# Two more feed-forward pairs by seven half-size products, and double scratch buffers between a pair's products

## The chip, the cores and the metric

The kernel runs on one core of one Trainium2 chip. The metric is the device time of one execution in microseconds (us); the median of three runs is 1425.7 us (1424.77 to 1426.21). The clock that the throttle granted to TensorE was 0.998 of full speed in the profiled execution.

## The reference

The program is a two-layer encoder trunk on 512 tokens of width 1024, in float32. Each layer is a mixer (attention in layer 0, an mLSTM in layer 1), a cross-attention to 256 memory rows, and a gated feed-forward stage with a short convolution. The change lies in the feed-forward stage alone:

```python
D_FF = 256 * math.ceil(8 * D_MODEL / 3 / 256)      # 2816
FFN_CONV = 3

def conv_ffn(xn, w_up, conv_w, conv_b, w_down):
    h = causal_depthwise_conv(xn @ w_up, conv_w) + conv_b
    g, u = jnp.split(h, 2, axis=-1)
    return (jax.nn.gelu(g) * u) @ w_down

# in each of the two layers:
x = x + conv_ffn(rms_norm(x, ffn_norm[layer]), ffn_w_up[layer], ffn_conv_w[layer],
                 ffn_conv_b[layer], ffn_w_down[layer])
```

## The kernel before

**Precision.** Every large product is made of three matmuls (`mm3`, lines 334 to 342): weight and input are each split into a rounded high part and the remainder, and high times high, high times low and low times high are added in PSUM. The high part of a weight is a cast on ScalarE (`wh`, `s2h`, `s4h`, `a22h`), the remainder a subtraction on VectorE (`wl`, `s2l`, `s4l`, `a22l`), from a tile that a DMA filled (`raw`, `sa`, `ra`) or that VectorE added up (`sb`).

**The feed-forward stage** (`ffn_steps`) walks over 22 pairs. Pair p is block p of the gate half and block 22+p of the linear half of the up-projection, 128 columns each, over 1024 input rows and 512 tokens. A pair ends in `tail`: three-tap convolution (one `c` activation on ScalarE and two `c<-hs,vec,c` on VectorE for each half), gelu, the product of both halves, and the split of the result into `ah` and `al`. The result is multiplied with the down-projection in chunks of 4, 4, 4, 4 and 6 pairs (`down`, tile `w`); from pair 5 on, two such down-products stand between a pair's own products (`fill`).

**Two ways to make a pair.** `plain` computes two blocks of 8 x 3 matmuls with 512 columns each, and VectorE scales each block on its way out (`hs<-acc,rb`). `seven` sees the pair as a product of 2 x 2 half-size blocks (two weight blocks, each in two halves of 512 rows, against two halves of the rows and of the tokens) and makes it from seven products instead of eight: each has 4 x 3 matmuls with 256 columns. It needs sums of weight blocks. The sum of the two weight blocks, `sa`, is made by a load from SP and an accumulating DMA from GpSimd onto it; `sb` is a sum on VectorE, onto which a second accumulating DMA adds once its split is made. It also needs sums of the input's blocks, `th` and `tl`, formed once a layer during pairs 0 and 1 (`forms`). Between the products, partial sums are taken out of PSUM: ScalarE copies the first product's bank to `v` and, after two more products have been added in that bank, to `u2` and `u3` (both are called `u` in the profile); VectorE adds these to other banks to get the four quarters of `hs`; one operation (`hs<-hs,rb`) then scales the whole pair. In the order of the code the seven are p1 (bank Y), p2 (X), p6 (onto Y), p5 (R), p7 (onto Y), p4 (onto Y), p3 (onto R). p6 needs `v` copied, p7 needs `u2`, p4 needs `u3`, and p3 needs the quarter that is made from `u3` and R.

**Order.** `Sched` is a planner: it is given each step with an engine, a duration, its inputs and the buffers that it takes, runs a timetable by its own durations, and issues the steps in that order. The order on VectorE and ScalarE is then fixed; the other engines take the instructions as issued. A name such as `v=1` in the planner's table is the count of buffers that it reckons with; the same count stands where the tile is made (`bufs`). `hs` has two buffers, `c` one, `sa` three, `sb` two, the weight parts `wh` and `wl` three.

Of the kernel before, what the change touches and what calls it, by code (L numbers as in the profile page):

```python
# [16 lines left out]
P = 128  # L17
# [5 lines left out]
NPAIR = DFF // P  # L23
CHUNKS = [(0, 4), (4, 4), (8, 4), (12, 4), (16, 6)]

SEVEN = (range(4, 22), range(4, 22))
EPS = 1e-6

X_AT, X_STEP = 2.6, 0.6
# [38 lines left out]
def folded(ap):  # L68

    return ap.rearrange("p (r k) -> p r k", r=2)  # L70
# [13 lines left out]
class Plan:  # L84
# [11 lines left out]
    def add(self, fn, dur=0.0, deps=(), prio=None, take=(), free=(), chain=(), pre=(), after=0.0, order=(), load=(), st=None):  # L96
        it = Item(fn, dur, [d for d in deps if d is not None], len(self.items) if prio is None else prio, take, free, chain, pre, after, order, load, st)
        it.n = len(self.items)
        self.items.append(it)
        return it  # L100
# [188 lines left out]
class Builder:  # L289
# [22 lines left out]
    def bank(self, tag):  # L312
        tag, bufs = BANKS[tag]
        return self.til(self.aux, tag, bufs=bufs)
# [918 lines left out]
    def ffn_steps(self, layer, mp):  # L1233
# [1 line left out]


        nc, t = self.nc, self.t
        sc = Sched(raw=3, h=3, s2=1, s4=1, a22=1, sa=3, sb=2, ra=2, hs=2, c=1, ft=2, v=1, u2=1, u3=1, act=10, acc=4, s=2, w=2)
        add = sc.add
        tt = lambda n: 0.055 + 1.06e-3 * n  # L1240
        act = lambda n: 0.1 + 0.83e-3 * n
# [195 lines left out]
        def seven(p, fill):  # L1437
            st, sa, sb, r2, f1, f3, s2, s4, a22 = ({} for _ in range(9))
# [57 lines left out]
            get = rows(st, at + 2.0)  # L1496

            def copied(tag, scale):
                st[tag] = self.til(mp, tag, (P, 256), bufs=1)
                nc.scalar.activation(folded(st[tag][:]), bank("Y")(), AF.Copy, scale=scale)  # L1500

            def sum_(out, a, b, op):
# [4 lines left out]
            hs = lambda j, l: (lambda: folded(st["hs_"][:, j, 2 + 256 * l : 258 + 256 * l]))  # L1507
            AC = 0.42
            p1 = pe(n, lambda: opened("Y", by, "acc", f3, 0, *X(0, 0), "Y", True), [w3], [("acc", by)])
            v = add("ACT", AC, lambda: copied("v", 1.0), [p1], clock[0], [("v", bv)])  # L1510
            p2 = pe(n, lambda: opened("X", bx, "acc", f3, 512, *X(1, 0), "X", True), [w3], [("acc", bx)], [("h", f3)])
            c11 = add("DVE", 0.33, lambda: sum_(hs(0, 0), bank("X"), tmp("v"), ALU.add), [p2, v, get], clock[0] + 2.0, (), [("acc", bx), ("v", bv)])
            p6 = pe(n, lambda: product(s2, 0, *T2, "Y", False), [w2, v, *formed], (), [("s2", s2)])
            u2 = add("ACT", AC, lambda: copied("u2", 1.0), [p6], clock[0], [("u2", bu2)])
            fill()
            p5 = pe(n, lambda: opened("R", br, "s", f1, 512, *T1, "R", True), [w1], [("s", br)])
            p7 = pe(n, lambda: product(f1, 0, *T3, "Y", False), [u2, w1], (), [("h", f1)])
            u3 = add("ACT", AC, lambda: copied("u3", -1.0), [p7], clock[0], [("u3", bu3)])
            c22 = add("DVE", 0.33, lambda: sum_(hs(1, 1), tmp("u3"), bank("R"), ALU.subtract), [u3, p5, get], clock[0], (), [("u3", bu3)])
            fill()  # L1520
# [52 lines left out]
        for p in range(22):  # L1573
            if p in due:
                queue += [(due[p], m) for m in range(8)]
            if p == 19:
                n = 6 if layer == 0 else 4
                queue, late = queue[:-n], queue[-n:]
            (seven if p in SEVEN[layer] else plain)(p, fill if p >= 5 else lambda: None)
            if p < 2:  # L1580
# [405 lines left out]
```

## Time and profile before

| what | value |
|---|---|
| median of 3 runs | 1425.7 us (1424.77 to 1426.21) |
| profiled execution | 1423.48 us, its span 1421.7 us |
| TensorE (PE) busy | 1403.3 us, 99% of the span |
| VectorE (DVE) busy | 1133.5 us, 80% |
| ScalarE (ACT) busy | 823.8 us, 58% |
| GpSimd (POOL) busy | 129.9 us, 9% |
| first matmul of the feed-forward of layer 0 / 1 | 397.37 us / 1085.38 us of the span |
| DMA | 190.02 MB, mean 134 GB/s |

PE's rows are matmuls, PEld's the weight loads beside them. Matmuls are pipelined, so the duration of one is longer than the distance to the next; the distance from start to start is what a matmul costs where nothing waits. The same holds for VectorE and ScalarE, where an instruction starts up to 0.1 us before the one ahead of it ends.

### The profile page before, as it was taken

To read this page: it belongs to the slowest core of one execution; us is meant where nothing else is said; L and a number is where in the kernel's file an instruction comes from. 1 tells how busy PE (TensorE), PEld (TensorE's weight loads), DVE (VectorE), ACT (ScalarE), POOL (GpSimd) and SP (SyncE) were. 2 spreads that over 40 slices of the span, in tenths; PEclk is the share of its full clock that TensorE was granted. 3 is DMA by queue.
4 is the path that set the end of the run, shared out by engine and by line. 5 is a ranking of instruction groups with operands and counts; after the bars stand their busy time and mean duration, and the time that the engine had idled before them with its cause. 6 is when DMAs were issued, how large, how long until landed. Compare 5 with 4: busy or idle time off the path is not lost.

```text
span 1421.7 us, 22241 instructions
## 1 busy us (share of the span) xinstructions
PE 1403.3 (99%) x8440; PEld 1262.9 (89%) x8440; DVE 1133.5 (80%) x1906; ACT 823.8 (58%) x1382; POOL 129.9 (9%) x189
## 2 busy tenths in 40 slices
PE   9999999999999999999999999999999999999998
PEld 7878788899889999999887788989988999999997
DVE  7778596666689999999768657667667999999984
ACT  7777574444476656566456654445445665656655
POOL 0001240000001111110001210000000111111000
PEclk9999999999999999999999999999999999999999
DMA  5233224323248777773233322323323886777522
GB/s 205 90 108 108 90 79 152 132 76 133 86 150 217 191 180 184 182 182 106 86 105 112 105 95 97 119 92 120 130 74 120 212 202 171 193 179 185 143 77 80
DMA packets 69211, 190.02 MB, mean 134 GB/s; under 512 B 7552, under 2 KB 7552, under 8 KB 69104
## 3 DMA queue, kind: packets, MB, share of 16 engines
q1 hardware_dynamic: 55648, 153.48, 32.3%
q0 software_dynamic: 12448, 34.00, 13.7%
q8 instruction: 66, 1.08, 0.3%
q10 hardware_dynamic: 1008, 1.12, 0.2%
q14 instruction: 41, 0.34, 0.1%
HBM read 186.43 MB, written 2.15 MB: 133 GB/s over the span
## 4 chain that ended last, share of the span: by engine, by line
PE 83%; DVE 8%; ACT 4%; issue 3%; DMA 1%; POOL 1%; SPq 0%; POOLq 0%; DVEq 0%; ACTq 0%
PE acc L340 16%; PE acc L341 16%; PE acc L342 16%; PE w L340 5%; PE w L342 5%; PE w L341 5%; PE s L340 3%; PE s L341 3%; PE s L342 3%; PE acc L402 2%; PE acc L404 2%; PE acc L403 2%; DVE wl L262 2%; DVE x L262 1%; PE w L1765 1%
## 5 line engine op out<-in xcount | busy, mean ns | idle before, releaser
L262 ACT CAST wh<-raw 128x1024 fp32r<-128x1024 f32 (+2 forms) x229 | 235.0, 1027 | 205.6 <-PE acc L341 118.8
L262 DVE TENSOR_TENSOR wl<-raw,wh 128x1024 fp32r<-128x1024 f32 (+2 forms) x229 | 274.2, 1198 | 38.7 <-ACT wh L262 38.2
L340 PE MATMUL acc<-xh,wh 128*128 128x512 f32 (+1 forms) x800 | 278.6, 348 | 0.8 <-ACT v L262 0.8
L341 PE MATMUL acc<-xl,wh 128*128 128x512 f32 (+1 forms) x800 | 274.0, 343 | 0.0
L342 PE MATMUL acc<-xh,wl 128*128 128x512 f32 (+1 forms) x800 | 273.6, 342 | 0.0
L340 PEld LDWEIGHTS acc<-xh,wh 128*128 128x128 f32 x800 | 152.5, 191 | 14.5 <-ACT v L262 1.2
L342 PEld LDWEIGHTS acc<-xh,wl 128*128 128x128 f32 x800 | 152.4, 190 | 13.9
L341 PEld LDWEIGHTS acc<-xl,wh 128*128 128x128 f32 x800 | 152.5, 191 | 13.2
L262 DVE SCALAR_TENSOR_TENSOR c<-hs,vec,c 128x512 f32<-128x512 f32 x176 | 131.8, 749 | 3.8 <-ACT c L262 0.8
L340 PE MATMUL w<-ah,wh 128*128 128x512 f32 x304 | 115.7, 381 | 0.2 <-ACT c L262 0.2
L342 PE MATMUL w<-ah,wl 128*128 128x512 f32 x304 | 115.2, 379 | 0.0
L341 PE MATMUL w<-al,wh 128*128 128x512 f32 x304 | 115.2, 379 | 0.0
L262 ACT ACTIVATE c<-hs,vec 128x512 f32<-128x512 f32 x88 | 70.8, 811 | 9.9 <-DVE hs L262 5.4
L262 ACT CAST ah<-c 128x512 fp32r<-128x512 f32 x44 | 27.2, 619 | 83.8 <-DVE c L262 83.8
L262 DVE TENSOR_TENSOR x<-acc,x 128x512 f32<-128x512 f32 (+1 forms) x43 | 28.1, 653 | 54.2 <-PE acc L342 53.4
L340 PEld LDWEIGHTS w<-ah,wh 128*128 128x128 f32 x304 | 57.6, 190 | 8.0 <-DVE x L262 0.9
L342 PEld LDWEIGHTS w<-ah,wl 128*128 128x128 f32 x304 | 57.5, 189 | 8.1
L341 PEld LDWEIGHTS w<-al,wh 128*128 128x128 f32 x304 | 57.6, 190 | 6.5
L342 PE MATMUL acc<-mem,wl 128*128 128x256 f32 (+1 forms) x192 | 59.9, 312 | 0.0
L340 PE MATMUL acc<-mem,wh 128*128 128x256 f32 (+1 forms) x192 | 59.6, 311 | 0.0
L341 PE MATMUL acc<-mem,wh 128*128 128x256 f32 (+1 forms) x192 | 59.6, 311 | 0.0
L1446 POOL DMA_DIRECT2D sa<-in_up_dram x36 | 30.8, 857 | 290.6 <-DMA sa<-in_up_dram 212.7
(357 smaller groups left out, 3750.5 us busy)
## 6 DMA issues: line engine op xcount, KB each, us to landing
raw<-in_up_dram SPq DMA_DIRECT2D x52, 512.0 KB, 3.7
sa<-in_up_dram SPq DMA_DIRECT2D x36, 512.0 KB, 3.4
sa<-in_up_dram POOLq DMA_DIRECT2D x36, 512.0 KB, 5.9
raw<-in_down_dram SPq DMA_DIRECT2D x32, 512.0 KB, 3.6
ra<-in_up_dram SPq DMA_DIRECT2D x36, 256.0 KB, 4.0
sb<-in_up_dram POOLq DMA_DIRECT2D x36, 256.0 KB, 4.9
raw<-in_xk_dram SPq DMA_DIRECT2D x16, 512.0 KB, 3.2
raw<-in_wo_dram SPq DMA_DIRECT2D x16, 512.0 KB, 3.3
```

The lines of the kernel that those rows point to most:

```text
L262: i = issue(*a, **k)
L340: mm(out, wh, xh, start=first, stop=False, skip_group_check=parts)
L341: mm(out, wh, xl, start=False, stop=False, skip_group_check=parts)
L342: mm(out, wl, xh, start=False, stop=last, skip_group_check=parts)
L402: mm(ps, xh[k][:, ts], wh, start=(k == 0), stop=False)
L403: mm(ps, xh[k][:, ts], wl, start=False, stop=False)
L404: mm(ps, xl[k][:, ts], wh, start=False, stop=(k == 7))
L1446: return add("POOL", 0.0029 * cols, lambda: nc.gpsimd.dma_start(out(), src(), accum_op=ALU.add), deps, due, (), (), 6.0)
L1765: nc.tensor.matmul(ps[:, lo:], vv[s][:, c], a[:], start=(s == 0), stop=(s == 3))
```

## The change

Pair 3 of both layers is made by `seven` instead of `plain`, so that pairs 3 to 21 are; pairs 0 to 2 stay. The tiles `v`, `u2` and `u3` get two buffers each, in the planner's table and where the tiles are made.

```diff
-SEVEN = (range(4, 22), range(4, 22))
+SEVEN = (range(3, 22), range(3, 22))
...
-        sc = Sched(raw=3, h=3, s2=1, s4=1, a22=1, sa=3, sb=2, ra=2, hs=2, c=1, ft=2, v=1, u2=1, u3=1, act=10, acc=4, s=2, w=2)
+        sc = Sched(raw=3, h=3, s2=1, s4=1, a22=1, sa=3, sb=2, ra=2, hs=2, c=1, ft=2, v=2, u2=2, u3=2, act=10, acc=4, s=2, w=2)
...
             def copied(tag, scale):
-                st[tag] = self.til(mp, tag, (P, 256), bufs=1)
+                st[tag] = self.til(mp, tag, (P, 256), bufs=2)
```

The planner makes a new order from this. It differs from the old one from pair 3 to about pair 10 of each layer and is the same everywhere else; the two layers change alike.

**PE, layer 0, from the end of pair 2 on.** Before, the rows are these, the first row of each product and the last of pair 2; `acc_907` and `acc_915` are the two plain blocks of pair 3, `acc_922`, `acc_926` and `s_4589` the banks Y, X and R of pair 4, `acc_939` the bank Y of pair 5.

```order
L342 MATMUL acc_899_4396<-xh_835_4097,wl_4319 128x512
L340 MATMUL acc_907_4441<-xh_794_3875,wh_4366 128x512
...
L340 MATMUL acc_915_4486<-xh_794_3875,wh_4412 128x512
...
L340 MATMUL acc_922_4528<-xh_794_3875,wh_4454 128x256
...
L340 MATMUL acc_926_4548<-xh_818_3993,wh_4454 128x256
...
L340 MATMUL acc_922_4528<-th_4110,s2h_4463 128x256
...
L340 MATMUL s_4589<-th_4110,wh_4500 128x256
```

After, `acc_906`, `acc_911` and `s_4497` are Y, X and R of pair 3, `acc_921`, `acc_928` and `s_4615` those of pair 4, and `acc_942` is Y of pair 5.

```order
L340 MATMUL acc_906_4437<-xh_794_3875,wh_4366 128x256
...
L340 MATMUL acc_911_4460<-xh_818_3993,wh_4366 128x256
...
L340 MATMUL acc_906_4437<-th_4110,s2h_4453 128x256
...
L340 MATMUL s_4497<-th_4110,wh_4434 128x256
...
L340 MATMUL acc_906_4437<-th_4110,wh_4434 128x256
...
L340 MATMUL acc_921_4534<-xh_794_3875,wh_4477 128x256
...
L340 MATMUL acc_928_4559<-xh_818_3993,wh_4477 128x256
...
L340 MATMUL acc_906_4437<-th_4110,a22h_4145 128x256
...
L340 MATMUL acc_921_4534<-th_4110,s2h_4550 128x256
...
L340 MATMUL s_4615<-th_4110,wh_4527 128x256
...
L340 MATMUL acc_942_4639<-xh_794_3875,wh_4556 128x256
```

The 48 matmuls of pair 3 with 512 columns have become 84 with 256, and the products of pairs 3, 4 and 5 stand interleaved: p4 of pair 3 comes behind p2 of pair 4. Behind the rows shown follow p7 of pair 4, p3 of pair 3 (with `s4h_4633`), p4 of pair 4, p2 of pair 5, p6 of pair 5 (`s2h_4672`), p5 of pair 5, p3 of pair 4 (`s4h_4732`), p7 of pair 5, p1 of pair 6 (`wh_4752`), p4 of pair 5, p2 of pair 6, and then the first two down-products.

**VectorE, the same place.** Before, behind the product of pair 1's halves (`c_4374`), the rows are these; `wl_4413` belongs to pair 3, `wl_4455`, `sb_4458`, `s2l_4464` and `wl_4501` to pair 4, `c_4460` to the tail of pair 2.

```order
L262 TENSOR_TENSOR wl_4413<-raw_4301,wh_4412 128x1024
L262 TENSOR_TENSOR al_4436<-c_4374,ah_4435 128x512
L262 TENSOR_TENSOR hs_4118<-acc_899_4396,rb_4259 128x512
L262 TENSOR_TENSOR sb_4458<-sa_4327,raw_4345 128x512
L262 TENSOR_TENSOR wl_4455<-raw_4345,wh_4454 128x1024
L262 SCALAR_TENSOR_TENSOR c_4460<-hs_4118,vec,c_4460 128x512 x2
L262 TENSOR_TENSOR s2l_4464<-sb_4458,s2h_4463 128x512
```

After, `sb_4432` comes first, and then these rows; `s2l_4454` and `wl_4435` belong to pair 3, `wl_4478`, `sb_4530`, `wl_4528` and `s2l_4551` to pair 4, `c_4457` to the tail of pair 2.

```order
L262 TENSOR_TENSOR al_4430<-c_4374,ah_4429 128x512
L262 TENSOR_TENSOR hs_4118<-acc_899_4396,rb_4259 128x512
L262 TENSOR_TENSOR s2l_4454<-sb_4432,s2h_4453 128x512
L262 TENSOR_TENSOR wl_4435<-sa_4327,wh_4434 128x1024
L262 TENSOR_TENSOR hs_4119<-acc_911_4460,v_4473 128x256
L262 SCALAR_TENSOR_TENSOR c_4457<-hs_4118,vec,c_4457 128x512 x2
L262 TENSOR_TENSOR wl_4478<-raw_4301,wh_4477 128x1024
L262 TENSOR_TENSOR sb_4530<-sa_4371,raw_4301 128x512
L262 SCALAR_TENSOR_TENSOR c_4457<-hs_4118,vec,c_4457 128x512 x2
L262 TENSOR_TENSOR wl_4528<-sa_4371,wh_4527 128x1024
L262 TENSOR_TENSOR hs_4119<-u_925_4553,s_4497 128x256
L262 TENSOR_TENSOR s2l_4551<-sb_4530,s2h_4550 128x512
```

`sa_4327` and `sa_4371`, which pairs 4 and 5 used, now serve pairs 3 and 4, and the splits of pair 4 stand among those of pair 3, ahead of the second half of pair 2's taps.

## The prediction

> **What bounds the kernel now.** I read the page's chain first, then the waits of PE, then busy times by stretches around pair 3, then the timelines of PE, VectorE and ScalarE there. The chain of work that ended last is PE's by 83%. Of PE's waits over the whole span two concern the lines of `mm3` (L340 to L342), and neither lies among the pairs: in the stretches from 397.6 to 660 us and from 1085.6 to 1400 us, which hold both stages but for layer 0's last down-products, the view lists no wait of PE.
>
> ```profile
> span 1421.7 us, 22241 instructions
> ...
> PE 83%; DVE 8%; ACT 4%; issue 3%; DMA 1%; POOL 1%; SPq 0%; POOLq 0%; DVEq 0%; ACTq 0%
> ```
>
> ```profile
> PE acc L340 <- ACT v L262: 0.8, 1, 0.8
> ...
> PE w L340 <- ACT c L262: 0.2, 1, 0.2
> ```
>
> The stretches (columns: length, then busy time of PE, PEld, DVE, ACT, POOL, granted clock, DMA share, GB/s) begin with pairs 0 to 2 of layer 0; the second is pair 3, the third pair 4 up to the first down-product, the last the steady state.
>
> ```profile
> 397.60:429.10 31.50, 31.50 (x151) 27.72 (x150) 30.68 (x51) 22.65 (x31) 2.98 (x3) 1.00 0.52 155
> 429.10:439.50 10.40, 10.40 (x50) 9.09 (x50) 10.24 (x15) 5.40 (x8) 1.74 (x2) 1.00 0.98 242
> 439.50:452.90 13.40, 13.40 (x122) 13.40 (x121) 12.95 (x20) 9.96 (x16) 2.57 (x3) 1.00 0.83 223
> ...
> 482.00:526.00 44.00, 44.00 (x328) 42.05 (x327) 41.40 (x59) 26.45 (x43) 5.21 (x6) 1.00 0.70 178
> 1085.60:1117.10 31.50, 31.50 (x151) 27.72 (x150) 30.68 (x51) 22.66 (x31) 2.93 (x3) 1.00 0.53 155
> 1117.10:1127.50 10.40, 10.40 (x50) 9.09 (x49) 10.24 (x15) 5.38 (x8) 1.72 (x2) 1.00 0.99 243
> ```
>
> PE is busy without a break, so the stage costs what its matmuls cost. But at pair 3 VectorE (10.24 of 10.40 us) and the DMA engines (0.98) are full too. The layers read alike, so I work out layer 0 and count it twice.
>
> **The change part by part. Matmuls.** These are the first matmuls of pair 3, of pair 4, of pair 4's second product and of its third.
>
> ```profile
> 429.13 0.38 PE L340 MATMUL acc<-xh,wh 128*128 128x512 f32 x1
> 439.49 0.27 PE L340 MATMUL acc<-xh,wh 128*128 128x256 f32 x1
> 440.82 0.28 PE L340 MATMUL acc<-xh,wh 128*128 128x256 f32 x1
> 442.16 0.28 PE L340 MATMUL acc<-th,s2h 128*128 128x256 f32 x1
> ```
>
> A plain pair takes 439.49 - 429.13 = 10.36 us for 48 matmuls (0.216 each). Two products of 12 take 442.16 - 439.49 = 2.67 us, one 1.335 (0.111 a matmul), seven 9.35. The change removes 48 and adds 84, which saves 10.36 - 9.35 = 1.0 us a layer, 2.0 us in all, if PE stays without a wait. A matmul with 256 columns costs more than half of one with 512, so an eighth less arithmetic saves only a tenth of the pair.
>
> [...] The rows above show 111 ns, so I take 2.0.
>
> **VectorE.** Its steps, from start to start, come from these rows of the place that the order lists show, and from rows of pair 4 in both layers.
>
> ```profile
> 423.36 1.22 DVE L262 TENSOR_TENSOR wl<-raw,wh 128x1024 fp32r<-128x1024 f32 x1
> ...
> 427.68 0.68 DVE L262 TENSOR_TENSOR c<-c 128x512 f32<-128x512 f32 x1
> 428.28 1.22 DVE L262 TENSOR_TENSOR wl<-raw,wh 128x1024 fp32r<-128x1024 f32 x1
> 429.41 0.69 DVE L262 TENSOR_TENSOR al<-c,ah 128x512 fp32r<-128x512 f32 x1
> 430.02 0.69 DVE L262 TENSOR_TENSOR hs<-acc,rb 128x512 f32<-128x512 f32 x1
> ...
> 432.35 1.54 DVE L262 SCALAR_TENSOR_TENSOR c<-hs,vec,c 128x512 f32<-128x512 f32 x2
> 433.80 0.68 DVE L262 TENSOR_TENSOR s2l<-sb,s2h 128x512 fp32r<-128x512 f32 x1
> ```
>
> ```profile
> 442.44 0.42 DVE L262 TENSOR_TENSOR hs<-acc,v 128x256 f32<-128x256 f32 x1
> 442.78 0.68 DVE L262 TENSOR_TENSOR s4l<-sb,s4h 128x512 fp32r<-128x512 f32 x1
> ```
>
> ```profile
> 1140.69 1.23 DVE L262 TENSOR_TENSOR hs<-hs,rb 128x1024 f32<-128x1024 f32 x1
> 1141.84 0.68 DVE L262 TENSOR_TENSOR a22l<-ra,a22h 128x512 fp32r<-128x512 f32 x1
> ```
>
> A split of 1024 costs 1.13 us, an operation on 512 0.60, two taps 1.45, a sum of 256 0.34, the scaling of a whole pair 1.15. Pair 3 loses two splits of 1024 and two `hs<-acc,rb` (3.46 us) and gains two splits of 1024, four operations on 512 (`sb`, `s2l`, `a22l`, `s4l`), three sums of 256 and one scaling, 6.83 us: 3.4 us more on a full engine, while PE needs the next pair 1.0 us sooner. Before, the last split for pair 3's first block began at 423.36 and took 1.22 us, done 4.55 us ahead of its use at 429.13; the change spends 4.4 us of such a lead. So I follow the new order by hand. PE starts pair 3 at 429.13 as before and takes 1.335 us a product: p1 429.13, p2 430.5, p6 431.8, p5 433.1, p7 434.5, then pair 4's p1 435.8, p2 437.1, pair 3's p4 438.5, pair 4's p6 439.8, p5 441.1.
>
> VectorE follows the old order up to 428.28. `sb_4432` ends its step at 428.9. `al_4430` waits for ScalarE's `ah`, so 429.6. The last plain `hs` ends at 430.2. `s2l_4454` waits for ScalarE's `s2h`, about 430.5, and is done at 431.1, p6 needs it at 431.8. `wl_4435` is done at 432.2 (p5: 433.1). A sum and two taps bring 434.0, `wl_4478` 435.2 (pair 4's p1: 435.8). `sb_4530` and two taps 437.2, `wl_4528` 438.4, a sum 438.7, `s2l_4551` 439.3 (p6: 439.8). The order goes on, up to `s4l_4733`, which p3 of pair 4 needs, with three splits of 1024 and one scaling (4.54), eight operations on 512 (4.8), three sums (1.0) and a tap (0.73), and I find 0.7 us of waits for ScalarE and PE in it: 451.1. That p3 is the seventeenth product after the first, 429.13 + 17 x 1.335 = 451.8. So all are in time, by 0.5 to 0.9 us. `al_4848`, which the first down-product takes with its fourth weight block, comes about 458.5 and is needed at 460.4. After that PE has two down-products a pair again and VectorE a margin, 41.40 of 44.00 us. I take a cost of nothing, the end to which the hand count points; the other end is B below. A gain is excluded here, since PE waits for nothing that could go.
>
> **ScalarE** gets 9 operations for 2 in a pair: three more splits of 512 and four copies.
>
> ```profile
> 428.40 0.62 ACT L262 CAST ah<-c 128x512 fp32r<-128x512 f32 x1 [3.15 <-DVE c L262]
> ...
> 441.16 0.36 ACT L262 ACTIVATE v<-acc 128x256 f32<-128x256 f32 x1
> 441.42 0.60 ACT L262 CAST s4h<-sb 128x512 fp32r<-128x512 f32 x1
> ```
>
> Three times 0.60 and four times 0.36 are 3.2 us, and it was busy for 5.40 of 10.40: covered. But PE now waits on it within a pair: `v_4473` is read from p1's bank after 430.6, behind a convolution step that ends about 431.1, and is out at 431.5, 0.3 us before p6 writes that bank. This is the thinnest of all margins.
>
> **The double buffers** free nothing that PE waited for before. What they allow is the new order: pair 4's `u2` is copied about 442.9, and pair 3's is still read by its last sum at about 446.7; in one buffer it could not be. Alone I cost them at nothing.
>
> **SP and POOL.** Each layer gets one `sa` load, one accumulation onto `sa`, one `ra` load and one accumulation onto `sb`, and loses one `raw` load; the transfers of pairs 4 and 5 now have to land sooner, as the products of pairs 3 to 5 overlap.
>
> ```profile
> q1 hardware_dynamic: 55648, 153.48, 32.3%
> q0 software_dynamic: 12448, 34.00, 13.7%
> ```
>
> ```profile
> sa<-in_up_dram POOLq DMA_DIRECT2D x36, 512.0 KB, 5.9
> ...
> sb<-in_up_dram POOLq DMA_DIRECT2D x36, 256.0 KB, 4.9
> ```
>
> The accumulation for `s4h_4732` can be issued when `s2l_4551` is done, 439.4; with 0.9 us of issue and 4.9 to land it is there at 445.2, and ScalarE takes it at 449.4: covered by 4 us. By the queue rows a transfer occupies all 16 engines for 2.99 us a MB from SP (32.3% of 1421.7 us for 153.48 MB) and 5.73 from GpSimd. A pair by `seven` moves 1.31 MB from SP and 0.79 from GpSimd, 8.4 us, and a load of down weights 1.6: 10.0 us where PE takes 9.35. Two such pairs stand in a row (3 and 4), 1.3 us late by perfect use, within the 4 us: nothing, if the transfers overlap as now.
>
> **The sum:** -2.0 us. The profiled execution took 1423.48 us (span 1421.7), 2.2 below the median of 1425.7; its own time would be 1421.5, the median 1423.7.
>
> **The rivals.** *VectorE is late and paces pairs 3 to 5 (B), slower than before.* For it: margins of 0.3 to 0.9 us after some 35 steps by hand, and a hand-over between engines costs more than I counted; where VectorE waited for a cast before, the row has 0.18 us.
>
> ```profile
> 440.55 1.23 DVE L262 TENSOR_TENSOR wl<-raw,wh 128x1024 fp32r<-128x1024 f32 x1 [0.18 <-ACT wh L262]
> ```
>
> Twelve operations between 428.3 and 451 take what ScalarE has just made; at 0.18 each that is 2.2 us. From 0.5 us on PE waits, at 1.5 the gain is gone, at the full 2.2 the stall is 1.7 a layer, 0.7 more than is saved: 1425.7 + 1.4 = 1427.1. Against it: most of these casts are finished well ahead of VectorE's turn.
>
> *GpSimd's queue serves one accumulation after the other (C), slower.* Place: pairs 3 to 5. A pair's two would take 5.9 + 4.9 us and 0.86 of issue each, 12.5 us, where PE takes 9.35: 3.2 late a pair, 9.5 after three; beyond the 4 us of cover PE waits, 5.5 us, less 1.0, in both layers: 1425.7 + 9.0 = 1434.7. It speaks for it that the DMA engines are full at pair 3; against it that the second was issued right behind the first:
>
> ```profile
> 434.11 0.84 POOL L1446 DMA_DIRECT2D sa<-in_up_dram  x1 [7.68 <-DVE c L262]
> 434.78 1.06 POOL L1446 DMA_DIRECT2D sb<-in_up_dram  x1
> ```
>
> [...]
>
> ```profile
> L1446 POOL DMA_DIRECT2D sa<-in_up_dram x36: 837/854/958, 417.2 to 1323.4; - x36
> L1446 POOL DMA_DIRECT2D sb<-in_up_dram x36: 844/867/1062, 434.8 to 1357.0; - x36
> ```
>
> [...] That the change does not happen is excluded by the order lists: 84 rows stand for 48.
>
> **How the numbers follow.** The forecast has 0.62, B 0.2, C 0.06, D 0.04, unnamed things 0.08. A measurement of this kernel tells about 0.2% (2.85 us) from no change, so the forecast's own 2.0 us lies within that: faster is below 1422.85, slower above 1428.55. The three runs before lie 1.4 us apart; that scatter carries about a fifth of forecast and D below 1422.85, and with a little of the unnamed this makes 0.15 faster. Slower is C, the far end of B and some of the unnamed, 0.12. The rest, 0.73, is the same. The range holds the forecast and D with their scatter, and B to its full price: 1422.4 to 1427.1.
>
> **What would show it.** Right: the matmuls of pair 3 at 0.111 us from start to start, no wait of PE in pairs 3 to 10, everything behind the first feed-forward stage 1.0 us sooner and the end 2.0. B would show as waits of PE for `v`, `u`, `s2l` or `wl` in the 30 us after pair 3 begins; C as waits of ScalarE or VectorE for `sa` or `sb` there, and as accumulations that take over 8 us to land. I am wrong if stretches outside pairs 3 to 10 have changed their length.

## The result, and the profile after

The changed kernel takes 1428.16 us (median of 20 runs, 1425.2 to 1430.12), the kernel before on the same chip 1425.09 (20 runs): 1.0021 of before, 95% interval 1.0014 to 1.0027. It is slower by 3.1 us, where 2.0 us less was forecast; 1428.16 lies 1.1 us above the upper end of the range. The profiled execution took 1426.66 us, 3.2 more than that of before.

The page's span and the chain that ended last:

```profile
span 1424.9 us, 22377 instructions
...
PE 75%; DVE 12%; ACT 5%; issue 4%; DMA 3%; POOL 1%; POOLq 0%; DVEq 0%; SPq 0%; ACTq 0%
```

PE has 75% of the chain where it had 83%, VectorE 12% instead of 8 and DMA 3% instead of 1: the chain now runs through other engines more often. The matmuls do what was said. These are, in PE's timeline, the first matmul of pair 3's first product, of its second and of its third:

```profile
427.85 0.27 PE L340 MATMUL acc<-xh,wh 128*128 128x256 f32 x1
...
429.19 0.28 PE L340 MATMUL acc<-xh,wh 128*128 128x256 f32 x1
...
430.53 0.28 PE L340 MATMUL acc<-th,s2h 128*128 128x256 f32 x1
```

A product costs 1.34 us. (Both layers' feed-forward stages begin at slightly other times in each of these profiles, so times of day are compared within a profile only; here pair 3 begins 1.28 us sooner than in the profile of before.) The loss is in PE's waits. In layer 0's pairs (397.6 to 670 us) the view listed none before and lists two now (us in total, times, longest):

```profile
PE acc L340 <- ACT u L262: 0.8, 1, 0.8
PE s L340 <- DVE hs L262: 0.4, 1, 0.4
```

and in layer 1's (1085 to 1380 us) five:

```profile
PE acc L340 <- ACT u L262: 0.8, 2, 0.6
PE s L340 <- DVE hs L262: 0.8, 2, 0.4
PE s L342 <- DVE s4l L262: 0.2, 1, 0.2
```

The view shows less than a wait costs (0.8 us for the first wait above, where the distance from start to start, shown below, is 1.09 instead of 0.11). I added up, over all matmuls of a stage, what the distance from start to start is above 0.2157 us for 512 columns and 0.1115 for 256. Before, that excess is 0.3 us in layer 0's pairs and 0.4 in layer 1's, after 2.4 and 4.2: 5.9 us of waits against 2.0 saved. Some 1.5 of the 5.9 lie near 1350 us, outside pairs 3 to 10. The first 397 us, which the change does not touch, happened to have 1.3 less.

The stretches by busy time (length, PE, PEld, DVE, ACT, POOL, clock, DMA share, GB/s) show where. After, with pairs 3 to 5 in the first row and pairs 7 to 9 in the second:

```profile
437.30:459.00 21.70, 20.89 (x183) 20.52 (x183) 20.23 (x31) 14.68 (x28) 4.34 (x5) 1.00 0.99 264
...
482.00:506.00 24.00, 23.59 (x165) 21.89 (x165) 23.75 (x36) 14.69 (x24) 3.48 (x4) 1.00 0.79 208
```

and before, over the same times (its stage began 1.28 us later; moved by that, VectorE's two figures change by less than 0.1 us):

```profile
437.30:459.00 21.70, 21.70 (x171) 21.00 (x171) 21.09 (x31) 14.51 (x25) 3.45 (x4) 1.00 0.86 220
...
482.00:506.00 24.00, 24.00 (x173) 22.72 (x172) 22.78 (x33) 13.90 (x23) 2.62 (x3) 1.00 0.65 160
```

These are two different places. In the first the DMA engines are full (a share of 0.99), and VectorE is less busy than before (20.23 us, 21.09 before): it waits too. In the second VectorE is full, 23.75 of 24.00 us, and the DMA engines are not (0.79).

**The first place.** GpSimd issues, with what each waited for, and below ScalarE's rows at the landing:

```profile
440.21 0.85 POOL L1446 DMA_DIRECT2D sa<-in_up_dram  x1 [9.11 <-DVE wl L262]
440.79 1.15 POOL L1446 DMA_DIRECT2D sb<-in_up_dram  x1
442.71 0.86 POOL L1446 DMA_DIRECT2D sa<-in_up_dram  x1 [0.77 <-DMA sa<-in_up_dram]
445.63 0.88 POOL L1446 DMA_DIRECT2D sb<-in_up_dram  x1 [2.06 <-DVE hs L262]
```

```profile
449.58 0.62 ACT L262 CAST s4h<-sb 128x512 fp32r<-128x512 f32 x1 [1.49 <-DMA sb<-in_up_dram]
...
454.90 0.62 ACT L262 CAST s4h<-sb 128x512 fp32r<-128x512 f32 x1 [1.46 <-DMA sb<-in_up_dram]
455.42 0.38 ACT L262 ACTIVATE u<-acc 128x256 f32<-128x256 f32 x1
```

The two accumulations onto `sb`, of pairs 4 and 5, landed at 449.50 and 454.80, 8.7 and 9.2 us after their issue. The first was also issued late: `s2l` of pair 4 was done at 438.10, but ahead of it in GpSimd's order stood the accumulation onto the `sa` of pair 6 (440.21), which could not go before SP's load of that tile, issued at 431.15, had landed at 439.52. ScalarE stood 1.5 us before each `s4h` cast. The first cast costs PE little, 0.2 us at p3 of pair 4, near 451 us. The product that needs the second would have had time (it begins at 463.82); but `u` of pair 5 stands behind that cast in ScalarE's fixed order, and p4 of pair 5 needs `u`. In PE's timeline the last matmul ahead of the wait and the first two behind it:

```profile
454.76 0.28 PE L342 MATMUL acc<-xh,wl 128*128 128x256 f32 x1
455.85 0.38 PE L340 MATMUL acc<-th,a22h 128*128 128x256 f32 x1 [0.81 <-ACT u L262]
456.07 0.28 PE L341 MATMUL acc<-tl,a22h 128*128 128x256 f32 x1
```

1.09 us from start to start instead of 0.11, and 0.22 once more behind it. **The second place** looks alike, with VectorE's `hs<-u,s` standing behind two splits and an `sb` sum:

```profile
504.84 0.28 PE L342 MATMUL acc<-th,a22l 128*128 128x256 f32 x1
505.52 0.38 PE L340 MATMUL s<-xh,s4h 128*128 128x256 f32 x1 [0.41 <-DVE hs L262]
```

### The profile page after: what moved, and what is told of

It is laid out like the page before. It is cut to its first block, busy times and chain, and to the rows that moved or that the text cites. A ratio compares the mean times of both kernels' runs of the same rounds, so it can differ in the third digit from the quotient of the medians.

```text
span 1424.9 us, 22377 instructions
## 1 busy us (share of the span) xinstructions
PE 1403.4 (98%) x8512; PEld 1263.4 (89%) x8512; DVE 1136.4 (80%) x1918; ACT 825.9 (58%) x1396; POOL 134.2 (9%) x193
## 4 chain that ended last, share of the span: by engine, by line
PE 75%; DVE 12%; ACT 5%; issue 4%; DMA 3%; POOL 1%; POOLq 0%; DVEq 0%; SPq 0%; ACTq 0%
PE acc L340 15%; PE acc L341 15%; PE acc L342 15%; PE w L340 4%; PE w L342 4%; PE w L341 4%; DVE wl L262 3%; PE s L340 2%; PE s L341 2%; PE s L342 2%; PE acc L402 2%; PE acc L404 2%; PE acc L403 2%; DVE x L262 1%; DVE c L262 1%
## 5 line engine op out<-in xcount | busy, mean ns | idle before, releaser
L340 PE MATMUL acc<-xh,wh 128*128 128x512 f32 (+1 forms) x784 | 270.3, 345 | 0.7 <-ACT v L262 0.7
L341 PE MATMUL acc<-xl,wh 128*128 128x512 f32 (+1 forms) x784 | 265.8, 339 | 0.0
L342 PE MATMUL acc<-xh,wl 128*128 128x512 f32 (+1 forms) x784 | 265.5, 339 | 0.0
L340 PEld LDWEIGHTS acc<-xh,wh 128*128 128x128 f32 x784 | 149.2, 190 | 13.4 <-ACT v L262 1.1
L342 PEld LDWEIGHTS acc<-xh,wl 128*128 128x128 f32 x784 | 149.1, 190 | 13.0
L341 PEld LDWEIGHTS acc<-xl,wh 128*128 128x128 f32 x784 | 149.2, 190 | 12.3
```

The costliest lines, as they stand in the source:

```text
L340: mm(out, wh, xh, start=first, stop=False, skip_group_check=parts)
L341: mm(out, wh, xl, start=False, stop=False, skip_group_check=parts)
L342: mm(out, wl, xh, start=False, stop=last, skip_group_check=parts)
```

## The experiments

The theory: two shortages add, late landings behind pair 3 and a full VectorE up to pair 9. The rival at first: one of the two makes both waits, VectorE being late because `s4h` is, or the other way round.

### The buffers: without them (e1), and alone (e2)

e1 is the changed kernel with one buffer for each scratch tile:

```diff
-... v=2, u2=2, u3=2 ...
+... v=1, u2=1, u3=1 ...
-                st[tag] = self.til(mp, tag, (P, 256), bufs=2)
+                st[tag] = self.til(mp, tag, (P, 256), bufs=1)
```

> Pair 3 by seven products in both layers, v, u2 and u3 in one buffer each as before. Theory 1 (late accumulations hold ScalarE's queue): the planner may no longer run pair 4 into pair 3's last product, the transfers crowd less, PE's waits at 451 and 455 us shrink from 1.3 us a layer to under 0.5, and the time falls to about 1426. Theory 2 (VectorE is full from pair 3 to pair 9 and paces PE): VectorE has the same work, so about 1428 as with two buffers. If the buffers are what makes the overlap pay, the time is above 1429.

1431.52 us, 1.0049 of before (1.0036 to 1.0061). PE's waits in layer 0's pairs:

```profile
PE acc L340 <- ACT u L262: 1.0, 2, 0.6
PE w L342 <- DVE wl L262: 0.9, 1, 0.9
```

This is the third case, above 1429. With one buffer the planner makes another order, and PE waits at other places; so the buffers, with the order that they allow, are worth some 4 us (0.0028 of 1425; by the intervals 2 to 6) once pair 3 is made by seven. e2 is the other half of the change, the buffers with pair 3 plain.

> The kernel before with `v`, `u2` and `u3` in two buffers and pair 3 as before (plain); nothing is left out. Every engine's instructions stand in the order of before. The prediction costs the buffers alone at nothing: 0.999 to 1.001 of before. Rival: buffers at other places in SBUF cost or save something by themselves: outside that.

1424.21 us, 1.0003 (0.9994 to 1.0011): nothing that can be told from zero, as costed.

### Each shortage relieved: the accumulations (e4), the taps (e5), both (e6)

```diff
 e4, e6
-            b1 = onto(lambda: sa["sa"][:], lambda: A2, 1024, [b1], at - 16.0)
+            few = 64 if 5 <= p <= 8 else 1024
+            b1 = onto(lambda: sa["sa"][:, :few], lambda: A2[:, :few], 1024, [b1], at - 16.0)
 e5, e6
-                nc.vector.scalar_tensor_tensor(out=c, in0=hs()[:, j, n : n + 512], ...
+                few = 64 if n == 0 and 3 <= p <= 8 else 512
+                nc.vector.scalar_tensor_tensor(out=c[:, :few], in0=hs()[:, j, n : n + few], ...
```

> The changed kernel, but the accumulations onto sa of pairs 5 to 8 in both layers carry 64 columns in place of 1024 (this part of the weight sums is left out); the order on every engine stays. Theory 1: with the DMA engines relieved the accumulations onto sb of pairs 4 and 5 land in 5 to 6 us, not 8.7 and 9.2, ScalarE's two waits of 1.5 us on them go, and with them PE's waits near 451 and 455 us, 1.3 us a layer: 1428.2 - 2.6 = 1425.6. Theory 2: those waits go too, but PE then reaches the late VectorE sooner and the wait near 505 us grows from 0.6 to about 1.7 us a layer: 1428 again.

> The changed kernel, but the last tap of the convolution of pairs 3 to 8 works on 64 columns in place of 512 in both layers (this part of the convolution is left out), which frees VectorE of some 0.6 us twelve times a layer; the order on every engine stays. Theory 1: the waits near 451 and 455 us stay, 1.3 us a layer; only what VectorE itself costs, 0.8 to 1.0 us a layer near 496 and 505 us, goes: 1428.2 - 1.9 = 1426.3. Theory 2: all of PE's waits from pair 3 to pair 10 go, 4.5 us in both layers: 1423.7.

> The changed kernel with both reliefs: accumulations onto sa of pairs 5 to 8 of 64 columns, and the last tap of pairs 3 to 8 on 64 columns (both parts left out). By either theory no wait of PE is left in pairs 3 to 10 of both layers, and what remains is the saving of matmuls, 1.0 us a layer: 1425.1 - 2.0 = 1423.1, ratio to the kernel before 0.9986. If it stays above 1425, a third cause is at work.

The orders of all engines are those of the changed kernel. As ratios to before, the first theories had 1.0004 for e4 and 1.0008 for e5, the second ones 1.002 and 0.999. e4: 1424.8 us, 1.0008 (0.9999 to 1.0017). e5: 1424.87, 1.0006 (0.9997 to 1.0015). e6: 1422.3, 0.9985 (0.9976 to 0.9994). The first theories lie within the intervals, the second ones outside. PE's waits in layer 0's pairs, e4 first, then e5; e6 has none:

```profile
PE s L340 <- DVE hs L262: 0.4, 1, 0.4
```

```profile
PE acc L340 <- ACT u L262: 0.8, 1, 0.8
```

Each edit takes away its own wait and leaves the other. The landings onto `sb` from 428 to 500 us (shortest, median, longest), e4 first and then the changed kernel:

```profile
DMA to landing us min/median/max: 3.6/5.5/6.4
```

```profile
DMA to landing us min/median/max: 4.7/7.5/9.2
```

The first rival falls: neither wait makes the other. But they are not independent. Added up from start to start as above, VectorE's waits cost 0.8 and 1.0 us in the two layers of the changed kernel and 1.4 us in each layer of e4: a PE that no longer waits for the landings comes sooner to a VectorE that is as late as before, as e4's second theory had it, though by less. Above e6 the late landings alone cost 0.0021 (e5), VectorE's debt alone 0.0023 (e4), and both together 0.0036, less than the sum; the intervals, some 0.0009 each way, do not settle the difference. e4 takes bytes off the engines and out of GpSimd's queue at once, so it does not tell which of the two makes the landings late. e6 is the sum without waits, 1.0 us a layer, as the prediction had it for the matmuls.

### What makes the landings late: SP's bytes (h1)

The changed kernel with SP's `raw` loads of pairs 3 to 6 and the first chunk's down weights halved, the half that is there being read twice:

```diff
-            l2 = load(r2, "raw", A1, 1024, at - 12.0)
+            l2 = load(r2, "raw", A1[:, :512] if few else A1, 1024, at - 12.0)
...
+        twice = lambda raw: raw[:, :512].unsqueeze(1).to_broadcast([P, 2, 512])
```

> The changed kernel in which the `raw` loads of pairs 3 to 6 (SP) and the down weights of the first chunk (SP) carry 512 of their 1024 columns, and ScalarE and VectorE read those 512 twice: every engine's instructions and their order stay, GpSimd's accumulations stay whole, and SP moves 8 x 0.25 = 2 MB less a layer (left out: half of those weights). Theory 1 (the DMA engines are full, share 0.99 between 437.3 and 459.0 us, so the accumulations onto `sb` wait for SP's bytes): about 1 MB of the 2 lies ahead of the second late landing, 3 us at 2.99 us a MB, so the two landings of 8.7 and 9.2 us fall to 6 or 7, the waits of PE for `s4l` and `u` behind `s4h` go, and only VectorE's own waits stay: 1425.5, 1.0006 of before. Rival (GpSimd's queue serves its accumulations one after another, whatever SP moves; C of the prediction): the landings stay at 8.7 and 9.2 us and the time at 1428.2, 1.0021.

1426.98 us, 1.0025 (1.0013 to 1.0038). The queues (packets, MB, share of the 16 engines; q0 is GpSimd's, q1 SP's) in the stretch of 21.7 us from pair 4 on, first the changed kernel (437.3 to 459.0), then this one, whose stage began 1.85 us later (439.15 to 460.85):

```profile
q0 software_dynamic: 650, 1.76, 51.3%
q1 hardware_dynamic: 1819, 3.96, 47.9%
```

```profile
q0 software_dynamic: 859, 2.35, 63.7%
q1 hardware_dynamic: 1411, 2.89, 35.9%
```

The engines stayed full: what SP left free GpSimd's queue took, 2.35 MB instead of 1.76. The two landings fell only to 7.8 and 7.7 us; layer 0's wait for `u` was gone, layer 1's was not (0.7 us). The landings fell by about half of what the theory expected, and the time is that of the changed kernel within the intervals, as the rival had it. SP's bytes count, but less than I said: by these rows a MB of accumulation holds the 16 engines for 0.513 x 21.7 / 1.76 = 6.3 us, a MB of SP for 0.479 x 21.7 / 3.96 = 2.6. GpSimd's transfers landed in the order of their issue (the four shown above at 445.60, 449.50, 452.75 and 454.80), which fits a queue served in order but does not show it. How much of the delay is full engines and how much the order within GpSimd's queue is not settled.

### Another order: a later landing told to the planner (h3), and all figures (f3, g3)

```diff
 h3
-  ... deps, due, (), (), 6.0)
+  ... deps, due, (), (), 9.5 if 3 <= p <= 6 and cols == 512 else 6.0)
 f3 (changed kernel) and g3 (kernel before)
-  ... deps, due, (), (), 6.0)
+  ... deps, due, (), (), 9.5)
-        ACV, STT = 0.71, 0.66
+        ACV, STT = 0.71, 0.74
```

> The changed kernel in which the planner is told 9.5 us instead of 6.0 until the accumulation onto `sb` has landed, in pairs 3 to 6 alone; nothing is left out. On ScalarE `u` and `v` of pairs 4 and 5 then come ahead of the `s4h` cast that waited, and PE gets another order there. Theory 1 (the loss at 451 and 455 us is a matter of what is queued behind the late `s4h`): PE no longer waits for `u`, 1.3 us a layer come back, VectorE's debt stays: 1425.6, 1.0006 of before. Rival (the bytes are late whatever stands ahead): the product that takes `s4h` waits instead, 1427 to 1428.5, and VectorE may run out a little later with another order.

1427.93 us, 1.0031 (1.0019 to 1.0043). ScalarE takes `u` ahead of `s4h` now, and PE does not wait for `u` in layer 0 any more, but for the remainder of the same tile, and for VectorE:

```profile
PE s L342 <- DVE s4l L262: 0.6, 1, 0.6
PE s L340 <- DVE hs L262: 0.4, 1, 0.4
PE w L342 <- DVE wl L262: 0.2, 1, 0.2
```

The wait moved and the time did not fall, as the rival had it, but not for the rival's reason. The bytes behind that `s4h` landed at 457.21; the cast began at 459.64 and the split `s4l` at 463.21, each behind other work in its engine's new order. What PE waits for here is VectorE's and ScalarE's order, no longer the DMA.

> The changed kernel in which the planner reckons with 9.5 us instead of 6.0 for every accumulation and 0.74 us instead of 0.66 for every tap, as the trace has them under load; nothing is left out. All seven-product pairs get another order. Theory 1 (two resources are short at pairs 3 to 5, but the planner can place the work where they are not): no wait of PE in the pairs, 1422.5, 0.9986 of before. Rival (VectorE and the DMA engines lack the time there, so whatever order waits): 1425 to 1428.

> The kernel before with the same two figures for the planner; nothing is left out. PE does not wait in the pairs of the kernel before, so both theories expect no change: 1424 to 1425.5, 0.999 to 1.001 of before. What f3_both_known is below it is what pair 3 by seven products is worth under a planner that knows both figures.

f3: 1437.19 us, 1.0096 (1.0082 to 1.011); g3: 1423.63, 1.0001 (0.9993 to 1.001). Both theories were wrong on f3. Its order starts the first `sa` load of pair 3 at 418.40 us, 12.8 us ahead of pair 3's first matmul, where the changed kernel has 17.0 (410.83 and 427.85), and ScalarE takes that tile's cast after a gelu that waits for VectorE's taps:

```profile
PE s L340 <- ACT wh L262: 3.2, 1, 3.2
PE acc L342 <- DVE s2l L262: 0.6, 1, 0.6
PE acc L340 <- ACT wh L262: 0.5, 1, 0.5
```

Behind the long wait PE also ran slowly: the granted clock was 0.64 from 437.23 to 441.90 us (0.92 over 437.30 to 459.00, where the changed kernel has 1.00), and 0.53 from 1131.20 to 1134.85 behind layer 1's, of 2.9 us. Truer figures for two steps did not give a better order. g3 shows that the same figures cost nothing while pair 3 is plain.

### The same sums without accumulations (c1, c2)

For pairs 5 and 6, with nothing left out: GpSimd adds what lies in SBUF.

```diff
+ b1 = add("POOL", 1.1, lambda: psum(out=lo(), in0=r2["raw"][:, :512], in1=up(), op=ALU.add), [b1, l2], at - 9.0)
+ b1 = add("POOL", 1.1, lambda: psum(out=up(), in0=up(), in1=a22["ra"][:], op=ALU.add), [b1, l1], at - 8.0)
 c2 as well
-            b2 = add("DVE", tt(512), s2_, [b1, l2], at - 5.0, [("sb", sb)])
+            b2 = add("POOL", 1.1, s2_, [b1, l2], at - 5.0, [("sb", sb)])
```

> The changed kernel in which GpSimd makes `sa` of pairs 5 and 6 by two additions in SBUF (128x512 each, from `raw`, `ra` and half a load) instead of an accumulating DMA: nothing is left out, a layer moves 2 x 0.5 MB less by accumulation and 2 x 0.25 MB less by SP. Theory 1 (two causes; the first is that the accumulations onto `sb` land late behind the bytes of the accumulations onto `sa`): the landings near 441 and 446 us take 6 us or less, PE does not wait for `u` behind `s4h`, VectorE's debt stays: 1425, 1.0006 to 1.001 of before. Rival (GpSimd's additions take VectorE's time, or come late themselves): 1428 or more.

> As c1_pool_sa, and GpSimd makes the sums `sb` of pairs 5 and 6 too (one addition of 128x512 each), which takes 2 x 0.6 us from VectorE; nothing is left out. Theory 1 (two causes that add): the DMA's part goes as in c1_pool_sa and VectorE's debt shrinks by 1.2 us, so its waits near 496 and 505 us shrink too: 1423 to 1424, 0.999 to 0.9997 of before. Rival (additions on GpSimd slow VectorE, or delay `s2h`): 1427 or more.

c1: 1432.06 us, 1.0058 (1.0046 to 1.007). c2: 1434.83, 1.0095 (1.006 to 1.013). In c1 the landings onto `sb` are short (longest 5.2 us) and PE does not wait for `u`; that half of the theory holds. But VectorE became later. One of GpSimd's additions, and VectorE beside it:

```profile
438.33 1.62 POOL L1458 TENSOR_TENSOR sa<-raw,sa 128x512 f32<-128x512 f32 x1 [7.02 <-DVE s2l L262]
```

```profile
439.05 1.98 DVE L262 TENSOR_TENSOR wl<-raw,wh 128x1024 fp32r<-128x1024 f32 x1
...
443.36 1.22 DVE L262 TENSOR_TENSOR wl<-sa,wh 128x1024 fp32r<-128x1024 f32 x1
```

The split took 1.98 us beside the addition and 1.22 without; it ended at 441.03, 1.08 us after the addition (439.95). What held it up is not shown. On a full engine that is paid, and moving `sb` too (c2) takes 0.6 us from VectorE and puts more of these beside it. The rival was right.

### The changed kernel once more (a1)

> The changed kernel once more, nothing else. If the losses follow from its order and its transfers, the waits near 451, 455 and 505 us and their like in layer 1 are there again, and the time is 1.0021 of before. The waits of the first profile near 1350 to 1363 us hung on one `raw` load that took 7.5 us instead of 4.3 to land: if that was chance, they are absent and the span is 1.4 us shorter; if it belongs to the order, they are there again.

1426.53 us (7 runs, 1424.48 to 1431.19), 1.0021 (1.001 to 1.0032). Its profiled execution is the longest of the seven. The late waits of layer 1, near 1350 us, are absent. h3's profile has them again (1336 to 1360 us, `raw` loads of 7.3 and 8.1 us before them), no other profile has more than 0.2 us there: they come in some executions, and why is not shown. The wait for `u` of pair 5 is there and takes 3.7 us, since this time SP's `sa` load landed 10.0 us after its issue; GpSimd waited for it, and the accumulation onto `sb` stood behind:

```profile
440.81 0.86 POOL L1446 DMA_DIRECT2D sb<-in_up_dram  x1 [1.19 <-DVE c L262]
449.83 0.86 POOL L1446 DMA_DIRECT2D sa<-in_up_dram  x1 [8.16 <-DMA sa<-in_up_dram]
450.39 1.22 POOL L1446 DMA_DIRECT2D sb<-in_up_dram  x1
```

```profile
460.00 0.62 ACT L262 CAST s4h<-sb 128x512 fp32r<-128x512 f32 x1 [5.40 <-DMA sb<-in_up_dram]
460.52 0.38 ACT L262 ACTIVATE u<-acc 128x256 f32<-128x256 f32 x1
```

The place and the chain of causes stay, the size does not. The stretches behind that wait show something more (the column after POOL is the granted clock):

```profile
457.00:461.00 4.00, 0.33 (x4) 0.13 (x2) 1.89 (x3) 1.00 (x3) 0.00 (x0) 1.00 1.02 223
461.00:464.40 3.40, 3.40 (x16) 3.40 (x17) 2.30 (x5) 2.41 (x5) 0.00 (x0) 0.51 0.52 157
464.40:470.00 5.60, 5.60 (x32) 5.04 (x31) 4.45 (x6) 3.09 (x5) 0.87 (x1) 0.99 0.43 92
```

After 3.9 us without a matmul PE ran at a granted clock of 0.51 for 3.4 us.

## Why the prediction was wrong, step by step

- **Matmuls:** right. A product takes 1.34 us, and e6, where nothing waits, is 0.9985 of before: 2.1 us, with 2.0 worked out.
- **SP and POOL:** the step that failed first. The tile of `s4h_4732` was to be there at 445.2, "covered by 4 us", which is 443.9 in this profile, 1.28 us sooner; it landed at 449.50, 5.6 us later. About half of that is the issue: I let it follow `s2l_4551` at once, which was done when I had said (438.1 here), but it came at 440.79, behind the accumulation for pair 6. The other half is the landing: 8.7 us, where I had put 0.9 and 4.9 (the 4.9, the median of all 36, counts from the start of the issue, so that the 0.9 stood in it twice). ScalarE was ready at 448.1, which is the 449.4 of the hand count, and idled 1.49 us. I had the engines' work (10.0 us in 9.35 a pair) and let two such pairs be 1.3 us late, but started them with empty engines, though the row of pair 3 showed a share of 0.98 before any pair was added. The larger loss came from a tile that I had not followed, that of pair 5, which took 9.2 us to land. I had asked only who uses a late tile. What is queued behind its cast, `u`, was needed sooner. Price: about 1.3 us in layer 0 and 1.4 in layer 1 in the first profile, over 5 us in layer 0 of the second.
- **VectorE:** the hand count was right as far as it went. `s2l_4454`, `wl_4435`, `wl_4478` and `s2l_4551` came 0.5 to 0.8 us ahead of their products, with 0.5 to 0.9 worked out. Wrong was the sentence that VectorE has a margin again once two down-products stand in a pair. Full at pair 3, it is still full at pairs 7 to 9 (23.75 of 24.00 us), and the debt is paid there: 0.8 to 1.0 us a layer, none of it owed to the landings, since e4 has it without them (1.4). The 41.40 of 44.00 us of before is the room in which a debt is worked off, 2.6 us in 44, and 3.4 us more were put in.
- **`v_4473`, called the thinnest margin:** no wait there.
- **The double buffers alone:** nothing, right (e2). That they are what makes the rest bearable (4 us, e1) I had not priced.
- **The rivals:** B had the right engine, but the wrong place (pairs 3 to 5 instead of 7 to 9) and price (1.7 us a layer). C's signs came, landings over 8 us and a wait for `sb`, at a quarter of its price of 5.5 us a layer in the first profile. I had set them against each other; each was too small alone to end past the range, and they came together. D was a larger saving by a shorter step of the matmuls: no run shows such a step as what a matmul costs. The rows show 0.111 us from start to start, and e6 saved 2.1 us.
- **Stretches outside pairs 3 to 10:** one did change, layer 1's near 1350 us, in one of the two profiles of the changed kernel, by some 1.5 us. That is about as much as the first 397 us happened to have less, so the 3.2 us between the profiles is near the medians' 3.1 partly by luck.

## What to carry to other kernels

A transfer's cover has to be reckoned with its landing under the load that the change makes, from the busiest stretch of the trace and with what is queued there already, not with the median of the run (8.7 and 9.2 us here, against 4.9); and its issue with what stands ahead of it on the engine that issues it. On engines with a fixed order, ask of every late input not only who needs it, but what stands behind its first user. Taking away one of two waits can lengthen the other (1.4 us a layer in e4, from 0.8 and 1.0), so measure them together as well as one by one. An engine that a change fills stays full until its margin has worked off the debt (here VectorE, from pair 3 to pairs 7 to 9), so follow its order to the point where the sum of the margins is larger than what was added.

## What the runs showed of the hardware that I had not expected

- A short wait of PE costs more than the wait: the matmul behind it takes 0.21 to 0.22 us instead of 0.11, behind each of the seven waits that the views of the changed kernel list above. After 3.9 us without a matmul (a1) the granted clock was 0.51 for 3.4 us, with 0.21 us from one 256-column matmul to the next; that cost another 1.6 us (16 matmuls, 0.10 each). In f3 the clock was 0.64 and 0.53 behind waits of 3.2 and 2.9 us. The length of the wait alone does not tell: near 155 us, ahead of the stages, the clock was 0.51 for 3.5 us behind a wait of 2.50 us in the profile of before, and 1.00 behind one of 3.04 in the changed kernel's. What sets it is not shown.
- An accumulating DMA held the engines 2.4 times as long a MB as a load of SP (6.3 against 2.6 us) where they were full, and 1.9 times over the whole run of before (5.73 against 2.99).
- An addition of 128x512 in float32 took GpSimd 1.6 us, VectorE 0.6. Beside one of GpSimd's (c1) a VectorE split took 1.98 us instead of 1.22, and beside another (448.56 to 450.32 us) a tap 1.45 instead of 0.75, while the sum `hs<-u,s` just ahead of that tap took 0.41, as elsewhere.
